# Rotary embedding in an attention stage: partner channels by transfers within SBUF in place of a product with a constant matrix

## The chip, the core and the metric

The kernel runs on one core of a Trainium2 chip. The metric is the time of one execution on the device in microseconds; lower is better. Line numbers are those of the kernel before.

The engines go by their names here: TensorE (PE in the profile) multiplies matrices and writes PSUM, VectorE (DVE) and GpSimd (POOL) work elementwise, ScalarE (ACT) evaluates functions and copies, SyncE (SP) issues most of the DMA transfers. Each engine has one queue and works it in order.

## What is computed

One program runs two blocks of a network on 512 tokens of 1024 channels. The first has an RWKV mixer, a gated delta rule mixer and two dense feed-forward layers. The second has a state-space mixer, a mixture of 32 experts, a dilated windowed attention and a second mixture of 32 experts, each followed by a layer norm. The change lies in the attention. There three groups of eight heads with 64 channels attend in windows; the groups with dilation read the tokens in a strided order. The queries and keys are first rotated in their lowest 16 channels:

```python
def _apply_partial_rope(t, cos, sin):
    half = ROPE_DIM // 2                       # ROPE_DIM = 16 of 64 channels
    t1, t2, rest = t[..., :half], t[..., half:ROPE_DIM], t[..., ROPE_DIM:]
    return jnp.concatenate([t1 * cos - t2 * sin, t2 * cos + t1 * sin, rest], -1)

def _dilated_attention_mixer(x, cos, sin, w_qkv, w_o):
    qkv = (x @ w_qkv).reshape(bsz, s, ATT_N_GROUPS, 3, ATT_HEADS_PER_GROUP, ATT_HEAD_DIM)
    for g, (window, dilation) in enumerate(ATT_PATTERNS):   # (128, 1), (512, 4), (2048, 16)
        q = _apply_partial_rope(qkv[:, :, g, 0], cos, sin)
        k = _apply_partial_rope(qkv[:, :, g, 1], cos, sin)
        o, m, l = _dilated_window_attention(q, k, qkv[:, :, g, 2], window, dilation)
        ...
```

So channel c below 8 needs its partner c + 8 with a minus sign, channel c from 8 to 15 its partner c - 8, and the other 48 channels stay as they are.

## The kernel before

The program is written in a tile framework: the Python code lists instructions in an order, and a scheduler of the framework then places them in the five queues, by the order of the listing and by when it expects operands and buffers to be ready. It also sets all semaphores. Loops are unrolled, except one in each expert layer.

Channels lie on the 128 partitions, so that a tile of 128x512 holds two heads for all 512 tokens. The attention (`attn`, from L1681) makes four passes `proj(p)`, p from 0 to 3, one for each pair of heads in each group. A pass has nine blocks, for the groups 1, 2, 0 in this order, and within each for v, q and k (f = 2, 0, 1). A block is one product of the weights' 128 columns with the 512 tokens, 24 matmuls on TensorE (`block`, the matmuls at L394): weights and tokens are each split into a high and a low part, and three of the four products of parts are kept. ScalarE evicts the finished block to SBUF (`qs`, L1744; L1746 for the group that is not strided). What is done with it is put off into a list `pend` and taken up within the next block, after its third step: for q and k the rotation `rope`, for v four transposes (`vnat`).

A rotation is: a product of the evicted tile with the constant 128x128 matrix `rot` on TensorE, which brings to each channel its partner with the right sign and zero to the others (L1712); a multiplication of the tile by the cosine table on GpSimd (L1715); a multiplication of the product by the sine table on VectorE (L1717) and the sum on VectorE (L1718). Outside the 16 channels the angle is zero. The tables are built once by `rope_tables` on VectorE and ScalarE while the expert layer before ends; two more copies hold them in the strided order (L1705).

`softmax(p)` makes the scores of pass p in four steps: two for the groups 1 and 2 (s = 0), then two for group 0 (s = 1). A step adds the mask (L1760) and the scores (L1767, L1770) in PSUM, takes the maximum on VectorE (L1781), exponentials on ScalarE (L1787), transposes on TensorE (L1797), copies these back on VectorE or ScalarE (L1801, L1799) and multiplies by v (L1812). `merge` lists softmax(p) interleaved with proj(p + 1), in proportion to the costs that the calls are given and that the generators yield.

Between proj(0) and softmax(0) there stands `affine` (L588): the gain and the offset of the last layer norm are applied to the residual, 128x1024 at a time, by eight operations on VectorE (L600), whose gain row is loaded on SyncE's queue (L598) into a buffer of split weights. There too the attention masks are loaded (L336), and VectorE copies them as bf16 (`wmask`, L1882).

Weights come by `Stream`: 512 KB per block on SyncE's queue (L234) into three raw buffers, split by ScalarE (L380) and VectorE (L381) into five buffers each of `wh` and `wl`. A load waits until a split has freed its raw buffer, and a split waits until TensorE has freed its buffer, some blocks ahead of use. Behind the attention's weights the same stream brings those of the second expert layer, whose six further buffers lie where the attention's tiles lay.

Of the kernel before, what the change touches and what calls it, by code (L numbers as in the profile page):

```python
# [9 lines left out]
F32 = mybir.dt.float32  # L10
F32R = mybir.dt.float32r
BF = mybir.dt.bfloat16
I32 = mybir.dt.int32
AF = mybir.ActivationFunctionType
ALU = mybir.AluOpType
# [4 lines left out]
P = 128  # L20
# [264 lines left out]
class Net:  # L285
# [43 lines left out]
        self.gar = c.tile([P, D], F32, name="gar")  # L329
        self.gate = None  # L330

    def load_hc(self, pool, first, end):

        a, b = HC_OFFS[first][0], HC_OFFS[end][0]
        t = pool.tile([P, b - a], F32, name="hc_" + first)
        self.nc.scalar.dma_start(t, self.ins["hc"][:, a:b])  # L336
        for n, (o, w) in HC_OFFS.items():
            if a <= o and o + w <= b and w:
                self.hct[n] = t[:, o - a:o - a + w]
# [1314 lines left out]
    def rope_tables(self, pool, tp):  # L1654

        V, A, nc = self.nc.vector, self.nc.scalar, self.nc
        pi = tp.tile([P, T], I32, name="posi", tag="qs", bufs=2)
        nc.sync.dma_start(pi, bcast_rows(self.ins["positions_2"][0]))
        ang = tp.tile([P, T], F32, name="ang", tag="qs", bufs=2)
        V.tensor_copy(ang, pi)  # L1660
        V.tensor_scalar(ang, ang, self.hcv("freq"), None, op0=ALU.mult)

        k = tp.tile([P, T], F32, name="angk", tag="qr", bufs=2)
        magic = 1.5 * 2.0 ** 23
        V.tensor_scalar(k, ang, 1.0 / (2 * math.pi), None, op0=ALU.mult)
        V.tensor_scalar(k, k, magic, None, op0=ALU.add)
        V.tensor_scalar(k, k, -magic, None, op0=ALU.add)
        rest = 2 * math.pi
        for bits in (5, 13, 21, None):
            c = float(np.float32(rest)) if bits is None else math.floor(rest * 2.0 ** bits) / 2.0 ** bits  # L1670
            rest -= c
            V.scalar_tensor_tensor(ang, k, -c, ang, op0=ALU.mult, op1=ALU.add)
        V.tensor_scalar(ang, ang, 3.1415925, -3.1415925, op0=ALU.min, op1=ALU.max)
        sin, cos = (pool.tile([P, T], F32, name=n) for n in ("sin", "cos"))
        A.activation(sin, ang, AF.Sin)
        V.scalar_tensor_tensor(k, ang, -1.0, ang, op0=ALU.mult, op1=ALU.max)
        V.tensor_scalar(k, k, -1.0, math.pi / 2, op0=ALU.mult, op1=ALU.add)
        A.activation(cos, k, AF.Sin)
        return cos, sin

    def attn(self):  # L1681
# [6 lines left out]
        with self.phase() as pool:  # L1688
# [10 lines left out]
            m4 = lambda a: a.rearrange("p (n b) -> p b n", b=4)  # L1699

            toks = lambda a, i: a[:, i * P:(i + 1) * P]
            tables = [(cos, sin)]
            tables.append([cn.tile([P, T], F32, name=n) for n in ("cos4", "sin4")])
            for a, b in zip(tables[1], tables[0]):
# [2 lines left out]
            def proj(p):  # L1707
                d, pend = X[p], []

                def rope(g, f, qs):  # L1710
                    pr = self.acc()
                    PE.matmul(pr, lhsT=self.hcv("rot"), rhs=qs, start=True, stop=True)  # L1712
                    qc = tp.tile([P, T], F32, name="qr")
                    c, s = tables[g > 0]
                    G.tensor_tensor(qc, qs, c, op=ALU.mult)  # L1715
                    q = d[f, g] = xp.tile([P, T], F32, name=f"qk{f}{g}")
                    V.tensor_tensor(q, pr, s, op=ALU.mult)  # L1717
                    V.tensor_tensor(q, q, qc, op=ALU.add)  # L1718

                def vnat(g, vs):  # L1720
                    pv = self.acc([P, 4, P])
# [5 lines left out]
                for g in (1, 2, 0):  # L1727
                    for f in (2, 0, 1):
                        g_ = self.block()
                        for n in range(NK + 1):  # L1730
                            try:
                                yield next(g_)
                            except StopIteration as e:
                                ps = e.value
                                break
                            if n == 2 and pend:
                                pend.pop()()
                                yield 900
                        while len(pend):
                            pend.pop()()  # L1740
                            yield 900
                        qs = tp.tile([P, T], F32, name="qs")
                        if g:
                            self.last_act = A.activation(qs.rearrange("p (b n) -> p b n", b=4), m4(ps), AF.Copy).ins  # L1744
                        else:
                            self.last_act = A.activation(qs, ps, AF.Copy).ins  # L1746
                        pend.append((lambda g=g, qs=qs: vnat(g, qs)) if f == 2 else (lambda g=g, f=f, qs=qs: rope(g, f, qs)))
                pend.pop()()
                yield 900

            def softmax(p):

# [124 lines left out]

            drain(proj(0))
            self.affine(lambda: self.wsp.tile([P, D], F32, name="row", tag="wl"))
            with self.phase() as p2, self.tc.issue_after(self.last_act):  # L1880
                self.load_hc(p2("at_m"), "attn0", "rot")
                V.tensor_copy(f2(mask), self.hcv("wmask"))  # L1882
            for p in range(4):
                work = [(softmax(p), 4 * 3600)]
                if p < 3:
                    work.append((proj(p + 1), 9 * 6100))
                if p == 2:
                    work.append((combine(0, 2), 10000))
                if p == 3:
# [721 lines left out]
```

## Time and profile before

| | us |
|---|---|
| median of three runs | 3793.52 |
| lowest and highest of these | 3785.03, 3798.27 |
| the profiled execution | 3798.41 |
| span of its instructions | 3796.6 |
| TensorE busy | 3556.3 |
| VectorE busy | 1900.4 |
| ScalarE busy | 1151.8 |
| GpSimd busy | 470.4 |

A profile is of one execution. Busy time of TensorE counts matmuls that overlap, with modelled ends; a busy TensorE is not one at its peak. A row of stretches gives start and end, length, then the busy time and the instructions of PE, PEld (its weight loads), DVE, ACT and POOL, then PEclk, the busy share of the DMA engines and GB/s. "Idle before" of a group is the time in which its engine did nothing just ahead of it. The chain of waits follows the end of a stretch back, at each step to what released the instruction or to the one before it on its engine. PEclk is TensorE's granted clock as a share of 2.4 GHz, the upper of its two levels; the lower is 1.2 GHz.

### The profile page before, as it was taken

What the parts mean: (1) busy time and instruction counts of PE and PEld (TensorE: products, weight loads), DVE (VectorE), ACT (ScalarE), POOL (GpSimd) and SP (SyncE); (2) the same over time, 40 slices, a digit from 0 to 9 for tenths busy, and PEclk for the clock granted to TensorE, in tenths of its full rate; (3) what the DMA queues carried; (4) which work ended last, traced back from release to release, by engine and by line L of the source; (5) the groups of instructions that cost most, each with busy time, mean ns of one, the idle gap of its engine ahead of it and who ended that gap; (6) DMA issues with size and microseconds to landing.
All of it is one profiled execution on the core that took longest, in us unless ns stands there. A gap on an engine that the chain in (4) does not pass through costs nothing. (4 is left out here: it accounts for less than half of the span.)

```text
span 3796.6 us, 53463 instructions
## 1 busy us (share of the span) xinstructions
PE 3556.3 (94%) x21818; PEld 2428.2 (64%) x21818; DVE 1900.4 (50%) x3437; ACT 1151.8 (30%) x2216; POOL 470.4 (12%) x300
## 2 busy tenths in 40 slices
PE   7999998999989998999989998999998999899998
PEld 5766656888776655888868777454546777444443
DVE  6766656533575555644489975222225345322223
ACT  4544433322443333422244432111114333211111
POOL 0111113201111111012131110200001111200001
PEclk9999998999998988999999999999999999899999
DMA  6323343322221102332243453999993224698897
GB/s 235 122 88 122 139 157 134 106 90 99 89 76 40 40 31 65 100 101 89 90 95 112 144 177 124 391 420 375 419 392 93 67 67 151 262 414 329 370 419 298
DMA packets 271342, 676.91 MB, mean 178 GB/s; under 512 B 25549, under 2 KB 164646, under 8 KB 222966
## 3 DMA queue, kind: packets, MB, share of 16 engines
q1 hardware_dynamic: 262342, 667.25, 47.4%
q0 software_dynamic: 928, 3.15, 0.6%
q10 hardware_dynamic: 7824, 3.06, 0.3%
q8 instruction: 173, 2.83, 0.3%
q14 instruction: 75, 0.61, 0.1%
HBM read 660.92 MB, written 12.48 MB: 177 GB/s over the span
## 5 line engine op out<-in xcount | busy, mean ns | idle before, releaser
L381 DVE TENSOR_TENSOR wl<-raw,wh 128x1024 fp32r<-128x1024 f32 x305 | 410.4, 1347 | 407.9 <-ACT wh L380 403.0
L380 ACT ACTIVATE wh<-raw 128x1024 fp32r<-128x1024 f32 x305 | 320.4, 1052 | 807.9 <-PE acc L394 380.1
L394 PE MATMUL acc<-uh,wh 128*128 128x512 f32 x1384 | 558.7, 406 | 2.5 <-ACT uh L380 2.5
L394 PE MATMUL acc<-ul,wh 128*128 128x512 f32 x1384 | 541.3, 391 | 0.0
L394 PE MATMUL acc<-uh,wl 128*128 128x512 f32 x1384 | 540.9, 391 | 0.0
L2083 PE MATMUL acc<-raw,xg 128*64 128x512 f32 x2048 | 449.3, 593 | 7.5 <-DMA raw<-in_moe_w_up_dram 7.5
L2083 PEld LDWEIGHTS acc<-raw,xg 128*64 128x64 f32 x2048 | 147.4, 137 | 300.1 <-issue 275.9
L394 PEld LDWEIGHTS acc<-uh,wh 128*128 128x128 f32 x1384 | 260.8, 189 | 65.5 <-issue 11.3
L394 PEld LDWEIGHTS acc<-ul,wh 128*128 128x128 f32 x1384 | 260.9, 188 | 56.9 <-issue 6.4
L394 PEld LDWEIGHTS acc<-uh,wl 128*128 128x128 f32 x1384 | 260.5, 188 | 56.1 <-issue 0.8
L2083 PE MATMUL acc<-raw,hT 128*64 128x512 f32 x1024 | 233.6, 601 | 3.3 <-issue 2.1
L257 POOL TENSOR_TENSOR raw<-raw,gar 128x1024 f32<-128x1024 f32 x60 | 154.3, 2590 | 616.1 <-DMA raw<-in_ffn_w_out_dram 425.9
L2204 DVE TENSOR_TENSOR h<-h,acc 128x512 f32<-128x512 f32 x32 | 22.0, 688 | 399.9 <-PE acc L2083 399.9
L386 POOL TENSOR_TENSOR rs<-rs,mhalf 128x1 f32<-128x1 f32 x32 | 19.3, 605 | 1169.8 <-DVE rs L385 741.7
L2083 PEld LDWEIGHTS acc<-raw,hT 128*64 128x64 f32 x1024 | 71.9, 138 | 140.6 <-issue 136.9
L2195 DVE SCALAR_TENSOR_TENSOR mrow<-acc,sg,mrow 128x512 fp32r<-128x512 f32 x64 | 47.9, 750 | 199.9 <-ACT mrow L2194 196.6
L394 PE MATMUL tp<-uh,wh 128*128 128x512 f32 x312 | 139.3, 446 | 0.0
L445 PE MATMUL o<-wh,hl 128*128 128x512 f32 x352 | 138.7, 394 | 0.0
L445 PE MATMUL o<-wh,hh 128*128 128x512 f32 x352 | 138.3, 393 | 0.0
L445 PE MATMUL o<-wl,hh 128*128 128x512 f32 x352 | 136.6, 388 | 0.0
L394 PE MATMUL tp<-uh,wl 128*128 128x512 f32 x312 | 134.9, 432 | 0.0
L394 PE MATMUL tp<-ul,wh 128*128 128x512 f32 x312 | 134.6, 431 | 0.0
(664 smaller groups left out, 6235.9 us busy)
## 6 DMA issues: line engine op xcount, KB each, us to landing
raw<-in_moe_w_up_dram SPq DMA_DIRECT2D x128, 1024.0 KB
raw<-in_moe_w_gate_dram SPq DMA_DIRECT2D x126, 1024.0 KB
raw<-in_moe_w_down_dram SPq DMA_DIRECT2D x74, 1024.0 KB
raw<-in_moe_w_down_dram SPq DMA_DIRECT2D x108, 512.0 KB
raw<-in_ada_w_dram SPq DMA_DIRECT2D x48, 1024.0 KB
raw<-in_ffn_w_in_dram SPq DMA_DIRECT2D x44, 1024.0 KB
raw<-in_ffn_w_out_dram SPq DMA_DIRECT2D x20, 1024.0 KB
raw<-in_attn_w_qkv_dram SPq DMA_DIRECT2D x36, 512.0 KB
```

The lines of the kernel that those rows point to most:

```text
L257: n.nc.gpsimd.tensor_mul(src, src, row[:, None, :].to_broadcast(list(src.shape)))
L380: self.nc.scalar.activation(dst_h, src, AF.Copy)
L381: self.last_split = self.nc.vector.tensor_sub(dst_l, src, dst_h.bitcast(F32)).ins
L386: self.pow_ins = self.nc.gpsimd.tensor_tensor(out, out, self.mhalf[:, :out.shape[1]], op=ALU.pow).ins
L394: self.nc.tensor.matmul(ps, lhsT=l[:, k], rhs=r[:, k], start=n == 0, stop=n == 3 * NK - 1)
L445: self.nc.tensor.matmul(ps, lhsT=l[:, kx0 + k, ts], rhs=r[:, k], start=start and n == 0, stop=stop and n == 5)
L2083: self.tc.keep_in_program_order(PE.matmul(*a, **k))
L2195: V.scalar_tensor_tensor(yl[:, cs], y[half], g, yh[:, cs].bitcast(F32), op0=ALU.mult, op1=ALU.subtract)
L2204: V.tensor_tensor(to(h), to(h), of(pu), op=ALU.mult)
```

## The change

The rotation's product with `rot` goes. In its place four transfers on SyncE's queue copy, within SBUF, the 8 partitions of each half of the rotated channels of each head to where the partner is: 8 rows of 512 floats, 16 KB each. Their target is one of two tiles `turned`, cleared once by GpSimd, so that the other channels stay zero. The sign goes into the sine table: the product of `rot` with a column of ones gives each channel's sign, and VectorE multiplies the table by it. The cosine product is written to the result's tile at once, and its own two buffers go. The rotation is no longer put off but listed right behind the eviction, and only v's transposes stay in `pend`. The evicted tile has three buffers, not two; the angles of the tables share them. The masks are loaded into a buffer of the transposed probabilities, not into a pool of their own. The cost given for a pass to `merge` is changed.

```diff
--- before.py
+++ after.py
@@ -329,10 +329,10 @@
         self.gar = c.tile([P, D], F32, name="gar")
         self.gate = None
 
-    def load_hc(self, pool, first, end):
+    def load_hc(self, pool, first, end, **k):
 
         a, b = HC_OFFS[first][0], HC_OFFS[end][0]
-        t = pool.tile([P, b - a], F32, name="hc_" + first)
+        t = pool.tile([P, b - a], F32, name="hc_" + first, **k)
         self.nc.scalar.dma_start(t, self.ins["hc"][:, a:b])
         for n, (o, w) in HC_OFFS.items():
             if a <= o and o + w <= b and w:
@@ -1654,13 +1654,13 @@
     def rope_tables(self, pool, tp):
 
         V, A, nc = self.nc.vector, self.nc.scalar, self.nc
-        pi = tp.tile([P, T], I32, name="posi", tag="qs", bufs=2)
+        pi = tp.tile([P, T], I32, name="posi", tag="qs", bufs=3)
         nc.sync.dma_start(pi, bcast_rows(self.ins["positions_2"][0]))
-        ang = tp.tile([P, T], F32, name="ang", tag="qs", bufs=2)
+        ang = tp.tile([P, T], F32, name="ang", tag="qs", bufs=3)
         V.tensor_copy(ang, pi)
         V.tensor_scalar(ang, ang, self.hcv("freq"), None, op0=ALU.mult)
 
-        k = tp.tile([P, T], F32, name="angk", tag="qr", bufs=2)
+        k = tp.tile([P, T], F32, name="angk", tag="qs", bufs=3)
         magic = 1.5 * 2.0 ** 23
         V.tensor_scalar(k, ang, 1.0 / (2 * math.pi), None, op0=ALU.mult)
         V.tensor_scalar(k, k, magic, None, op0=ALU.add)
@@ -1673,6 +1673,13 @@
         V.tensor_scalar(ang, ang, 3.1415925, -3.1415925, op0=ALU.min, op1=ALU.max)
         sin, cos = (pool.tile([P, T], F32, name=n) for n in ("sin", "cos"))
         A.activation(sin, ang, AF.Sin)
+
+        one, sign = (pool.tile([P, 1], F32, name=n) for n in ("one", "sign"))
+        V.memset(one, 1.0)
+        ps = self.tp([P, 1])
+        nc.tensor.matmul(ps, lhsT=self.hcv("rot"), rhs=one, start=True, stop=True)
+        V.tensor_copy(sign, ps)
+        V.tensor_scalar(sin, sin, sign, None, op0=ALU.mult)
         V.scalar_tensor_tensor(k, ang, -1.0, ang, op0=ALU.mult, op1=ALU.max)
         V.tensor_scalar(k, k, -1.0, math.pi / 2, op0=ALU.mult, op1=ALU.add)
         A.activation(cos, k, AF.Sin)
@@ -1699,6 +1706,11 @@
             m4 = lambda a: a.rearrange("p (n b) -> p b n", b=4)
 
             toks = lambda a, i: a[:, i * P:(i + 1) * P]
+
+            turned = [cn.tile([P, T], F32, name=f"turned{i}") for i in range(2)]
+            for z in turned:
+                G.memset(z, 0.0)
+            turned = itertools.cycle(turned)
             tables = [(cos, sin)]
             tables.append([cn.tile([P, T], F32, name=n) for n in ("cos4", "sin4")])
             for a, b in zip(tables[1], tables[0]):
@@ -1708,14 +1720,15 @@
                 d, pend = X[p], []
 
                 def rope(g, f, qs):
-                    pr = self.acc()
-                    PE.matmul(pr, lhsT=self.hcv("rot"), rhs=qs, start=True, stop=True)
-                    qc = tp.tile([P, T], F32, name="qr")
+                    pr = next(turned)
+                    for r in (0, 64):
+                        for a, b in ((r, r + 8), (r + 8, r)):
+                            nc.sync.dma_start(pr[a:a + 8], qs[b:b + 8])
                     c, s = tables[g > 0]
-                    G.tensor_tensor(qc, qs, c, op=ALU.mult)
                     q = d[f, g] = xp.tile([P, T], F32, name=f"qk{f}{g}")
-                    V.tensor_tensor(q, pr, s, op=ALU.mult)
-                    V.tensor_tensor(q, q, qc, op=ALU.add)
+                    G.tensor_tensor(q, qs, c, op=ALU.mult)
+                    V.tensor_tensor(pr, pr, s, op=ALU.mult)
+                    V.tensor_tensor(q, q, pr, op=ALU.add)
 
                 def vnat(g, vs):
                     pv = self.acc([P, 4, P])
@@ -1739,14 +1752,15 @@
                         while len(pend):
                             pend.pop()()
                             yield 900
-                        qs = tp.tile([P, T], F32, name="qs")
+                        qs = tp.tile([P, T], F32, name="qs", bufs=3)
                         if g:
                             self.last_act = A.activation(qs.rearrange("p (b n) -> p b n", b=4), m4(ps), AF.Copy).ins
                         else:
                             self.last_act = A.activation(qs, ps, AF.Copy).ins
-                        pend.append((lambda g=g, qs=qs: vnat(g, qs)) if f == 2 else (lambda g=g, f=f, qs=qs: rope(g, f, qs)))
-                pend.pop()()
-                yield 900
+                        if f == 2:
+                            pend.append(lambda g=g, qs=qs: vnat(g, qs))
+                        else:
+                            rope(g, f, qs)
 
             def softmax(p):
 
@@ -1877,13 +1891,13 @@
 
             drain(proj(0))
             self.affine(lambda: self.wsp.tile([P, D], F32, name="row", tag="wl"))
-            with self.phase() as p2, self.tc.issue_after(self.last_act):
-                self.load_hc(p2("at_m"), "attn0", "rot")
+            with self.tc.issue_after(self.last_act):
+                self.load_hc(tp, "attn0", "rot", tag="prT")
                 V.tensor_copy(f2(mask), self.hcv("wmask"))
             for p in range(4):
                 work = [(softmax(p), 4 * 3600)]
                 if p < 3:
-                    work.append((proj(p + 1), 9 * 6100))
+                    work.append((proj(p + 1), 9 * 5200 + 3 * 900))
                 if p == 2:
                     work.append((combine(0, 2), 10000))
                 if p == 3:
```

## Rows read from the trace of the kernel before

**Rows 1.** The page: its head, and busy time (share) and instructions by engine.
```profile
span 3796.6 us, 53463 instructions
...
PE 3556.3 (94%) x21818; PEld 2428.2 (64%) x21818; DVE 1900.4 (50%) x3437; ACT 1151.8 (30%) x2216; POOL 470.4 (12%) x300
```

**Rows 2.** Stretches by pass: busy us of each engine, granted clock, DMA share.
```profile
2892.00:2944.00 52.00, 45.27 (x194) 34.67 (x193) 27.88 (x29) 14.02 (x19) 11.07 (x7) 0.96 0.32 96
2944.00:3017.40 73.40, 72.00 (x385) 53.85 (x386) 26.65 (x42) 27.94 (x60) 9.04 (x6) 0.98 0.25 72
3017.40:3089.90 72.50, 71.91 (x395) 54.10 (x394) 27.89 (x51) 26.90 (x60) 10.39 (x7) 1.00 0.22 66
3089.90:3166.80 76.90, 76.90 (x461) 57.57 (x460) 36.05 (x63) 26.77 (x60) 11.43 (x7) 1.00 0.27 86
```

**Rows 3.** Groups by line, 2892 to 3166: count, busy us, mean ns, idle before.
```profile
L1715 POOL TENSOR_TENSOR qr<-qs,cos 128x512 f32<-128x512 f32 x24 | 41.4, 1727 | 237.6 <-ACT qs L1744 156.0 <-ACT qs L1746 63.5 <-DVE cst L1840 18.0
...
L1712 PE MATMUL acc<-qs,hc_rot 128*128 128x512 f32 x47 | 25.0, 611 | 3.4 <-ACT qs L1746 3.4
...
L1718 DVE TENSOR_TENSOR qk<-qk,qr 128x512 f32<-128x512 f32 x23 | 15.9, 690 | 1.6
L1717 DVE TENSOR_TENSOR qk<-acc,sin 128x512 f32<-128x512 f32 x23 | 15.8, 687 | 13.9 <-PE acc L1712 13.9
```

**Rows 4.** Chain of waits, 2892 to 2945: start, length, what stood on it.
```profile
2894.57 0.86 PE acc L1712 x2
...
2919.54 0.86 PE acc L1712 x2
...
2923.87 3.68 DMA row<-in_ln_g_dram
...
2943.97 1.03 PE acc L1760 x2
```

**Rows 5.** Chain of waits, 2944 to 3164: shares by line.
```profile
by line: PE acc L394 69.3%; PE acc L1712 7.2%; PE po L1812 5.2%; PE tp L1797 4.5%; PE acc L1767 3.4%; PE acc L1760 2.7%; PE acc L1770 2.6%; PE acc L1865 1.9%; PE acc L1723 1.8%; issue 0.7%; ACT qs L1746 0.5%; ACT wh L380 0.2%
```

**Rows 6.** TensorE's waits, 2944 to 3164: total us, times, longest.
```profile
PE acc L1760 <- DVE wmask L1882: 5.3, 1, 5.3
PE acc L1712 <- ACT qs L1746: 2.0, 2, 1.4
```

**Rows 7.** SyncE's DMA issues in order of time: early in the span, and near 3201.
```profile
275.04 0.33 SPq L1034 DMA_DIRECT2D od<-yT  x1
...
277.07 0.32 SPq L1040 DMA_DIRECT2D oback<-od  x1
...
3201.07 1.28 SPq L234 DMA_DIRECT2D raw<-in_moe_w_gate_dram  x3
```

**Rows 8.** Waits of SyncE's queue, 2850 to 3260: total us, times, longest.
```profile
SPq L234 <- DVE wl L381: 275.6, 38, 13.5
```

**Rows 9.** Timeline of pass three: first head's exponentials (ACT) and transposes (PE), two steps.
```profile
3021.52 0.47 ACT L1787 ACTIVATE pr<-acc,stat 128x256 f32<-128x256 f32 x1
...
3035.11 0.46 ACT L1787 ACTIVATE pr<-acc,stat 128x256 f32<-128x256 f32 x1
...
3025.12 0.60 PE L1797 MATMUL tp<-hc_ident,pr 128*128 128x128 f32 x4
...
3042.77 0.60 PE L1797 MATMUL tp<-hc_ident,pr 128*128 128x128 f32 x4
```

**Rows 10.** Line L1677: count, min/median/max ns, when.
```profile
L1677 DVE TENSOR_SCALAR angk<-angk x1: 430/430/430, 2881.0 to 2881.0; 128x512 f32<-128x512 f32 x1
```

**Rows 11.** Chain of waits behind the last block, 3155 to 3185.
```profile
3168.59 0.70 DVE qk L1718
3169.28 1.20 DVE stat L1781 x2
```

**Rows 12.** A stretch ahead of the experts, and the first expert product on TensorE.
```profile
3236.00:3246.00 10.00, 2.55 (x24) 2.33 (x23) 7.45 (x36) 0.42 (x2) 0.00 (x0) 0.50 0.00 1
...
3246.53 0.55 PE L2083 MATMUL tp<-mrow,ul 128*128 128x256 f32 x1 [1.96 <-DVE mrow L2088]
```


## The prediction

> **What bounds the kernel now.** First the page: the span is 3796.6 us in an execution of 3798.41 us, and TensorE is busy 94% of it, VectorE 50%, GpSimd 12% [rows 1]. Such a share is a mean over stages, so the next view is the table of stretches, cut where the attention stage starts a new pass [rows 2]. Attention runs from 2892 to about 3167 us. In its three passes with softmax beside projection (2944 to 3167) TensorE is busy 72.0 of 73.4, 71.9 of 72.5 and 76.9 of 76.9 us, at a granted clock of 0.98 to 1.00, which is the upper level of 2.4 GHz; VectorE has 27 to 36 us of work there and the DMA engines are a quarter full. In the first pass (2892 to 2944), which has no softmax beside it, TensorE is busy 45.3 of 52.0. So three passes are bound by TensorE, and work taken off it there shortens the kernel, while the first pass has another limit at its end. The chain of waits says the same and names the lines: for 2944 to 3164 it stands on TensorE nearly throughout, with 7.2% on L1712, the rotation product [rows 5]. For the first pass it goes along TensorE until 2923.87, then through the load of the norm's gain row (3.68 us) and VectorE, which applies gain and offset rows to the residual (eight operations), and comes back to TensorE at 2943.97 by way of the mask copy [rows 4].
>
> **What is removed.** 24 rotation products, six in each of four passes. The profile shows two records per product, of 0.61 us each [rows 3], but matmuls overlap; what one costs is its step on the chain, 0.86 us for its two records [rows 4]. In the first pass four of the six stand on the chain, 0.86 us each (the first and the last are shown), ahead of the gain row's load: 4 x 0.86 = 3.4 us. The load waits for a buffer that TensorE releases, so it moves with them. The last two stand beside VectorE's work and are worth nothing. In the three later passes the chain's own sum is 7.2% of the 220 us from 2944 to 3164, 15.8 us; this is 17 products, since the last one of pass four lies behind 3164. At the end of two of these passes TensorE also waits for the eviction that the last product reads, 2.0 us [rows 6]; the next instruction will be the mask product of the next scores, whose rotated channels come three blocks earlier. That makes 3.4 + 15.8 + 2.0 = 21.2 us.
>
> **What is added and moved.** (1) 96 transfers of 16 KB on SyncE's queue, four per rotation. No transfer within SBUF is in this trace. The nearest from below: a 256 KB store is issued at 275.04, and a load that reads it back follows at 277.07, after a wait, so landing takes 2.0 us with its issue [rows 7]. From above: the 512 KB gain row, 3.68 us [rows 4]. Issues follow each other by 1.28 / 3 = 0.43 us [rows 7]. So the last of four lands 3 x 0.43 + 2.0 = 3.3 us after the eviction, at most 1.3 + 3.7 = 5.0. I take 3.3, because a transfer of 16 KB is nearer to the smaller neighbour. With two VectorE operations of 0.69 us [rows 3] the rotated tile is there 4.7 to 6.4 us after its eviction. The first scores of a pass read groups 1 and 2, whose last rotation is three blocks (over 16 us of TensorE) earlier, and group 0 is read two score steps later still: the latency itself is hidden by projection work. If that cover were gone, it would cost its 4.7 us once per pass, 19 us.
> (2) SyncE works in order. A rotation's transfers wait for ACT's eviction; behind them stand weight loads, which now wait 275.6 us in all for VectorE's split to free a buffer [rows 8]. Splits run up to four blocks ahead of their use, so 1.7 us of issues in front of a load, 40 us in all, are covered. The other way round is worse: a load waiting for a split ahead of a rotation's transfers holds these back. In passes two to four splits follow evictions within about 1 us. At the end of pass one splits stand among the residual's work, and a rotation held there would hold the mask copy behind it.
> (3) VectorE keeps two operations per rotation. The first now reads SBUF alone; SBUF alone costs 690 ns and PSUM with SBUF 687 [rows 3], so nothing. But it waits for DMAs instead of TensorE, and behind it on VectorE may stand the maximum of the scores, which releases ACT's exponentials and then TensorE's transposes. In pass three the first head's exponentials end at 3021.99 and its transposes start at 3025.12, 3.1 us of slack; in the next step it is 3035.57 and 3042.77, 7.2 us [rows 9]. The longer slack covers even 5.0 us. The shorter one stands at the start of a pass, right behind the last rotation of the pass before. There VectorE would begin the maximum 3.3 + 1.4 = 4.7 us after that eviction, where TensorE's scores no longer wait for it; against 3.1 us of slack TensorE loses 1.6 us, in passes three and four together 3.2, if VectorE's order puts the rotation first, and nothing if it puts the maximum first. I take 2 us; the late end is 2 x (1.6 + 1.7) = 6.6.
> (4) GpSimd's multiplication stays the same, 1.73 us [rows 3] against one rotation every 12 us. Its two clearings of 128x512 come before the first rotation; GpSimd has almost nothing there.
> (5) The tables: one multiplication of the sine table by a sign, 0.43 us like L1677 [rows 10], a copy of one column and a one-column product. VectorE is on the chain there, so 0.6 us; between 0 and 2, if VectorE waits for the product among TensorE's other work.
> (6) Releasing the fifth accumulator, a third buffer for the evicted tile, and the planner's cost of 5200 for 6100 per block change no duration; they may shift where softmax work falls in between, less than a score step's slack either way.
> (7) Exit: behind the last block VectorE does the last rotation's two operations ahead of the score maximum, on the chain [rows 11]. If the maximum goes first, 1.3 us are won; if VectorE waits for the last transfer ahead of it, up to 1.4 are lost. I take zero.
> (8) The expert stage behind attention begins with its buffers full: DMA is idle from 3236 to 3246, and TensorE then waits for VectorE's one-hot rows, not for weights [rows 12]. All loads of that stage are released by what runs before them, so the gain is passed on whole.
>
> Sum: 21.2 - 2.0 - 0.6 = 18.6 us. From the profiled execution: 3798.4 - 18.6 = 3779.8. That execution lies 4.9 us over the median of the runs, 3793.5; the forecast for the median is 3775. Its own range is 3768 (all of 21.2 and 1.3 at the exit, with some scatter) to 3782 (21.2 less the late ends: 6.6, 2 and 1.4).
>
> The Trainium skill (DMA: Bandwidth & Descriptors, Rules for kernel authors) speaks against this change: many small transfers should be coalesced, since under 64 KB one pays mostly overhead. Its fixed cost of about 2 us per DMA (Anatomy of one DMA — SWDGE (gpsimd) path, stated for that queue) paid four times in a row would be an estimate of 8 us per rotation; no transfer within SBUF here shows it. By that rule the sum would turn over, as the last rival shows; the rows of issues that follow each other by 0.43 us speak for overlap [rows 7].
>
> **Rivals.** *The gain is mostly hidden, 3785, chance 0.20.* At the end of pass one SyncE has a load ahead that waits for a split behind the residual's work. The last rotation then comes after VectorE has done it, and the mask copy later: instead of winning 3.4 us, pass one loses about 4 (landing 3.3 and 0.7 for the operation), and the starts of passes three and four cost 5 rather than 2. That is 18.6 - 3.4 - 4 - 3 = 8 us left. For it: TensorE already waits 5.3 us there for the mask [rows 6]. Against it: TensorE reaches the last eviction some 5 us earlier, while VectorE's residual work takes as long as before, so the transfers have time.
> *Transfers held behind the next weight load, slower, 3841, chance 0.07.* Place: SyncE's queue in passes two to four, with each rotation's transfers ordered behind the load that waits for the next split. Price: a block lasts 72.5 / 9 = 8.1 us, so a rotation comes 8.1 + 2.0 = 10.1 us after its eviction, and VectorE, held all that time, has 27.9 + 6 x 10.1 = 88.5 us per pass of 72.5 [rows 2] and is the bound: 3 x 16 = 48 us slower. It decides from a hold of (72.5 - 5.2 - 27.9) / 6 = 6.6 us per rotation on, since 5.2 us is what TensorE saves per pass. For it: the queue already waits 275.6 us for splits [rows 8]. Against it: a rotation's transfers are ready a little before that split, so an order by readiness puts them first.
> *The four transfers go one after the other, slower, 3806, chance 0.04.* Then a rotation takes 4 x 2.03 = 8.1 us [rows 7], VectorE has 27.9 + 6 x 8.1 = 76.5 us per pass and again is the bound: 3 x 4.0 = 12 us slower. The rule of the skill above would be its ground.
> *The change doesn't do what it says* is not open for the products, which are gone from the program; it could only be that TensorE's order around them falls worse, which is in the range.
>
> **How the numbers follow.** Forecast 0.69, hidden 0.20, the two slower ones 0.11. Differences under 0.3%, 11.4 us, can't be told from none in this kernel. The forecast's range (11 to 26 us won) is faster: 0.69. The hidden case is within: 0.20. The rest is slower: 0.11. The range of 8 in 10 takes in forecast and hidden case with the runs' scatter of a few us: 3765 to 3795.
>
> **What would show it.** Right: L1712 is gone; TensorE stays busy over 98% of passes two to four, which last 5 to 6 us less each; the expert stage begins 18 us earlier and lasts as long; a rotation's transfers land 3 to 5 us after its eviction. Wrong: TensorE idle ahead of the transposes or the score products with VectorE named as the releaser; VectorE waiting long for the transfers; TensorE's wait for the mask far over 7 us. An end of attention earlier by 18 us with no gain at the end of the kernel would refute step (8).

## The result, and the profile after

The kernel after takes 3774.5 us (median of 20 runs, 3759.2 to 3798.3) against 3794.9 us for the kernel before, run beside it (20 runs, 3785.0 to 3809.2): a ratio of 0.995, 95% interval 0.9936 to 0.9964. The forecast was 3775. The profiled execution took 3775.04 us. Line numbers in the views below are those of the kernel that the view is of. First the page of the kernel after, the span and the busy time of the engines, which answers to [rows 1].

```profile
span 3773.2 us, 53604 instructions
...
PE 3530.8 (94%) x21772; PEld 2418.9 (64%) x21772; DVE 1902.0 (50%) x3440; ACT 1151.2 (31%) x2216; POOL 469.5 (12%) x302
```

TensorE has 46 records and 25.5 us less; VectorE and GpSimd are as before. The span is 23.4 us shorter, and not all of that is the change. TensorE's timeline shows in both traces where the last product of the expert layer before ends, where the first projection product and the mask products that open a pass stand, and where the first product of the expert layer behind attention stands. Cut there, the kernel after is 5.4 us ahead when attention begins (at 2853.42 and at 2848.06), wins 20.8 us in the attention stage, and takes 2.8 us longer in the experts behind it (550.1 and 552.8 us). The change does not touch the code of the first and the third stretch, and their lengths scatter by more than that among the runs below (2840 to 2870 us and 548 to 555 us). So the stage is the measure: 393.1 us before, 372.3 after.

Stretches of the kernel after, from mask product to mask product, with the columns of [rows 2]: stretch and length, busy time of PE, PEld, DVE, ACT, POOL, granted clock, DMA share, GB/s. The first is pass one.

```profile
2887.89:2934.89 47.00, 39.36 (x180) 32.23 (x178) 27.76 (x26) 13.77 (x19) 10.77 (x7) 0.97 0.40 115
2934.89:3002.43 67.54, 67.54 (x374) 52.16 (x375) 29.13 (x44) 26.53 (x59) 7.79 (x5) 0.97 0.28 80
3002.43:3068.10 65.67, 65.67 (x376) 50.88 (x375) 29.41 (x48) 26.75 (x60) 9.64 (x6) 1.00 0.28 79
3068.10:3139.10 71.00, 71.00 (x447) 54.96 (x446) 35.05 (x64) 28.02 (x62) 9.94 (x6) 1.00 0.29 88
```

In passes two to four TensorE has no idle time left: busy time equals length. Its clock is at the upper level but for the start of pass two, behind TensorE's wait at the end of pass one. The granted clock is 0.50 there, the lower level, for 3.16 us of work in the kernel before and for 4.20 us in the kernel after:

```profile
2943.97:2947.13 3.16, 3.16 (x19) 2.10 (x20) 1.16 (x2) 0.00 (x0) 0.00 (x0) 0.50 0.75 221
```

```profile
2934.89:2939.09 4.20, 4.20 (x21) 2.95 (x22) 4.10 (x6) 0.00 (x0) 0.00 (x0) 0.50 0.44 127
```

The four passes cut at the same events in the kernel before lasted 51.72, 73.91, 72.52 and 76.21 us. For the sum, the three passes and the exit are cut at the last projection product instead (3164.90 and 3139.26), before above and after below:

```profile
2943.97:3164.90 220.93, 218.93 (x1231) 164.35 (x1231) 89.60 (x151) 81.02 (x179) 29.73 (x17) 0.99 0.24 75
3164.90:3246.53 81.63, 66.43 (x452) 52.81 (x450) 48.52 (x135) 29.48 (x61) 10.44 (x9) 0.84 0.34 131
```

```profile
2934.89:3139.26 204.37, 204.37 (x1195) 158.12 (x1196) 93.74 (x154) 81.31 (x179) 27.37 (x17) 0.99 0.29 83
3139.26:3220.37 81.11, 65.36 (x450) 52.54 (x447) 48.11 (x136) 29.35 (x61) 10.28 (x9) 0.82 0.37 141
```

The passes are 16.6 us shorter: TensorE's busy time by 14.56 us, and its idle time by 2.00, from 2.00 to nothing. The chain of waits of 2935 to 3139, beside [rows 5], has lost L1712 and has no other engine on it at all:

```profile
by line: PE acc L394 75.8%; PE po L1826 5.6%; PE tp L1811 4.9%; PE acc L1781 3.7%; PE acc L1774 2.9%; PE acc L1784 2.8%; PE acc L1879 2.0%; PE acc L1736 1.9%; PE tp L1858 0.4%
```

The rotation itself, 2880 to 3140: GpSimd's product with the cosine, VectorE's two operations (count, busy us and mean ns, idle time ahead), answering to [rows 3].

```profile
L1729 POOL TENSOR_TENSOR qk<-qs,cos 128x512 f32<-128x512 f32 x23 | 37.5, 1631 | 216.6 <-ACT qs L1757 162.1 <-ACT qs L1759 54.5
L1730 DVE TENSOR_TENSOR turned<-turned,sin 128x512 f32<-128x512 f32 x23 | 17.0, 738 | 36.4 <-DMA turned<-qs 36.4
L1731 DVE TENSOR_TENSOR qk<-qk,turned 128x512 f32<-128x512 f32 x23 | 17.0, 738 | 2.1 <-DVE turned L1730 0.5
```

VectorE now waits 36.4 us for the transfers and TensorE for none of that. How soon they land is seen where VectorE waits for one: the eviction on ACT (start, length), the four issues on SyncE's queue, VectorE's operation with its wait in brackets.

```profile
2905.77 0.58 ACT L1757 ACTIVATE qs<-acc 128x512 f32<-128x512 f32 x1
```

```profile
2906.37 2.68 SPq L1726 DMA_DIRECT2D turned<-qs  x4
```

```profile
2910.50 0.69 DVE L1730 TENSOR_TENSOR turned<-turned,sin 128x512 f32<-128x512 f32 x1 [3.38 <-DMA turned<-qs]
```

From the eviction's end, 2906.35, to 2910.50 is 4.15 us (4.14 for the next one that waits). The issues follow each other by 2.68 / 4 = 0.67 us.

The end of pass one, the chain of waits (start, length), answering to [rows 4]:

```profile
2923.19 0.65 SPq L1726
...
2925.24 1.94 DMA turned<-qs
...
2927.59 4.57 DVE res L600 x3
2932.16 0.60 DVE turned L1730
...
2934.42 0.42 DVE wmask L1896
...
2934.89 1.04 PE acc L1774 x2
```

It ends as before, with the residual's operations, a rotation and the mask copy on VectorE. The chain also leads through a rotation's transfers (2923.19 to 2927.19), but they were no limit: VectorE was at work until 2927.6, and the pass is as long without them (no_transfers below). TensorE's wait there, and those of SyncE's queue (2850 to 3260: total us, times, longest), answering to [rows 6, 8]:

```profile
PE acc L1774 <- DVE wmask L1896: 7.6, 1, 7.6
```

```profile
SPq L234 <- DVE wl L381: 93.4, 17, 13.0
SPq L1726 <- ACT qs L1757: 76.6, 16, 8.3
```

The queue waits less for splits (275.6 us in [rows 8]), and it now waits for evictions as well.

### The profile page after: what moved, and what is told of

Same layout as the page of the kernel before. It is cut to its first block, busy times and chain, and to the rows that moved or that the text cites. A ratio compares the mean times of both kernels' runs of the same rounds, so it can differ in the third digit from the quotient of the medians.

```text
span 3773.2 us, 53604 instructions
## 1 busy us (share of the span) xinstructions
PE 3530.8 (94%) x21772; PEld 2418.9 (64%) x21772; DVE 1902.0 (50%) x3440; ACT 1151.2 (31%) x2216; POOL 469.5 (12%) x302
## 5 line engine op out<-in xcount | busy, mean ns | idle before, releaser
L2097 PE MATMUL tp<-mrow,ul 128*128 128x256 f32 x512 | 130.3, 294 | 4.0 <-DVE mrow L2102 4.0
```

The source lines that it names most:

```text
L2097: self.tc.keep_in_program_order(PE.matmul(*a, **k))
```

## The experiments

Attention by stretch in each profile, in us, cut at the same events. "Prologue" runs from the last expert product of the layer before to the first projection product, "exit" from the mask product that follows pass four to the first expert product.

| kernel | prologue | pass 1 | pass 2 | pass 3 | pass 4 | exit | stage | ratio to before, 95% |
|---|---|---|---|---|---|---|---|---|
| before | 38.8 | 51.7 | 73.9 | 72.5 | 76.2 | 79.9 | 393.1 | 1 |
| after | 39.8 | 47.0 | 67.5 | 65.7 | 71.0 | 81.3 | 372.3 | 0.9936 to 0.9964 |
| no_product | 38.1 | 47.0 | 67.6 | 65.5 | 71.0 | 81.8 | 370.9 | 0.9910 to 0.9958 |
| no_transfers | 39.4 | 46.9 | 67.3 | 65.7 | 71.0 | 81.2 | 371.4 | 0.9926 to 0.9971 |
| transfers_twice | 42.9 | 42.6 | 67.5 | 65.7 | 71.0 | 82.1 | 371.7 | 0.9912 to 0.9972 |
| product_too | 39.7 | 51.5 | 75.1 | 72.3 | 76.2 | 80.6 | 395.4 | 1.0002 to 1.0034 |
| two_queues | 40.1 | 46.6 | 67.7 | 65.7 | 71.0 | 81.1 | 372.2 | 0.9940 to 0.9976 |
| rows_four | 39.7 | 42.9 | 67.2 | 65.7 | 71.0 | 82.0 | 368.5 | 0.9919 to 0.9950 |
| mask_early | 40.8 | 39.2 | 69.3 | 65.7 | 71.0 | 81.1 | 367.0 | 0.9893 to 0.9945 |
| mask_and_queues | 42.9 | 39.2 | 69.2 | 65.7 | 71.0 | 81.0 | 368.9 | 0.9906 to 0.9952 |
| after_again | 40.5 | 47.3 | 67.5 | 65.7 | 71.0 | 81.2 | 373.1 | 0.9910 to 0.9953 |
| mask_early_again | 42.9 | 39.2 | 68.9 | 65.7 | 71.0 | 81.3 | 368.9 | 0.9917 to 0.9952 |
| transfers_four | 40.3 | 42.9 | | | | | 427.8 | 1.0082 to 1.0130 |

**Is it the product?** First the kernel before with the product left out, so that the sine term reads the evicted tile itself; its output lacks the swap of partner channels.

```
-                    pr = self.acc()
-                    PE.matmul(pr, lhsT=self.hcv("rot"), rhs=qs, start=True, stop=True)
...
-                    V.tensor_tensor(q, pr, s, op=ALU.mult)
+                    V.tensor_tensor(q, qs, s, op=ALU.mult)
```

> The kernel before without the rotation product (VectorE multiplies the evicted tile by the sine table in place of its partner, so the rotation is wrong; all else as before). Attention stage here: from the last product of the first expert layer to the first of the second, 393.1 us before, 372.3 after the change. Theory (the gain is TensorE's time for the products plus its waits at the passes' ends): stage 372 +- 2, time about 21 us under the kernel before. Rival (the gain comes from listing the rotation earlier, or from the fifth accumulator being free): stage stays above 385.

The passes are those of the kernel after within 0.2 us, with no transfer, no sign in the table and no third buffer, and with the rotation listed where it was. The accumulator that the product wrote is free here too, and no run separates the two; but in passes two to four of the kernel before TensorE waited for nothing except the evictions that the product reads, 2.0 us [rows 6], so there was no wait for an accumulator to win. Then the reverse: the kernel after, with the product run beside the transfers and its result unused.

```
                             rope(g, f, qs)
+                            pend.append(lambda qs=qs: PE.matmul(self.acc(), lhsT=self.hcv("rot"), rhs=qs, start=True, stop=True))
+                while len(pend):
+                    pend.pop()()
+                    yield 900
```

> The changed kernel with the product of the evicted tile and the constant matrix kept on TensorE beside the transfers, put off into the next block as before; nobody reads it. Theory: 0.86 us for each of the 21 or so that stand on the chain, so 18 to 22 us of the gain are lost, stage 390 to 395. Rival (the product was hidden, the gain came otherwise): stage within 5 us of 372.3.

All of the gain is gone: 75.1, 72.3 and 76.2 us, and the chain of 2948 to 3170 has the product's share back (L1764 is its line here; 7.2% in [rows 5]). The stage, 395.4 us, is 0.4 over my figure. That pass two is 1.2 us longer than before goes with the clock: the granted clock is 0.50 for its first 6.0 us, not for 3.2.

```profile
by line: PE acc L394 69.5%; PE acc L1764 7.1%; PE po L1830 5.2%; PE tp L1815 4.5%; PE acc L1785 3.4%; PE acc L1778 2.7%; PE acc L1788 2.6%; PE acc L1736 2.0%; PE acc L1883 1.8%; issue 0.7%; ACT qs L1759 0.5%; ACTq L1759 0.0%
```

**What do the transfers cost?** The kernel after without them (the partner tile stays zero), and with each of them issued twice.

```
-                    for r in (0, 64):
-                        for a, b in ((r, r + 8), (r + 8, r)):
-                            nc.sync.dma_start(pr[a:a + 8], qs[b:b + 8])
```

> The changed kernel without the 96 transfers (the turned tiles stay zero, so the sine part is left out). Theory (transfers are hidden except ahead of the mask copy at the end of pass one and at the exit): stage 4 to 6 us shorter than the changed kernel's 372.3, so 366 to 368; passes two to four 67.1, 65.7, 71.0 us from score product to score product change by under 1 us each. Rival (VectorE's 36 us of waiting for the transfers costs something in every pass): each of these passes 3 us shorter or more, stage 360 or less.

```
-                    for r in (0, 64):
+                    for r in (0, 64, 0, 64):
```

> The changed kernel with each of the four transfers made twice, so eight issues of 0.67 us and a landing of 1.9 us: the rotation waits 7.3 us for its partner, not 4.6. Theory (slack covers it inside the passes; the two ends pay 2.7 us each): stage 372.3 + 3 to 8, passes two to four within 1.5 us each. Rival (as the prediction had it: from a hold of 6.6 us per rotation VectorE becomes the bound, 27.9 + 6 x 7.3 = 71.7 us per pass): passes two to four 5 us longer each or more, stage 388 or more.

Without transfers the stage is 0.9 us shorter, about what the kernel after differs from itself (372.3 and 373.1); I had expected 4 to 6, so the holds that I priced are not there. With twice as many I had expected 3 to 8 us more; the stage is 0.6 shorter, although a rotation's partner now comes 7.1 us after its eviction. VectorE's wait for them (2885 to 3140) did not double, it fell:

```profile
DVE turned L1730 <- DMA turned<-qs: 9.8, 7, 3.8
```

VectorE's order had been made anew, with more of its other work ahead of each rotation. That shows in pass one too, where the residual's operations went behind the mask copy: VectorE has 13 us of work there, not 28, and 38 in pass two, not 29, and pass one is 4.4 us shorter.

```profile
2888.89:2931.53 42.64, 39.33 (x179) 32.22 (x178) 12.97 (x15) 13.77 (x19) 9.52 (x7) 1.00 0.38 96
2931.53:2998.99 67.46, 65.85 (x375) 50.87 (x375) 38.07 (x53) 27.20 (x59) 8.29 (x6) 1.00 0.39 105
```

Passes three and four are unchanged. Pass two has the length of the kernel after (67.5 us) by chance: its clock is at the upper level throughout, so that TensorE is busy for 1.7 us less, but it idles for 1.6 us. The chain of waits leads from there through an eviction, which stands on ScalarE behind the split of a late weight load, to the transfers ahead of that load on SyncE's queue. So the doubled transfers did cost something once, by the queue and not by VectorE:

```profile
2934.93 0.62 SPq L1726
...
2936.10 5.68 DMA raw<-in_attn_w_qkv_dram
...
2942.82 0.59 ACT qs L1757
...
2943.46 0.66 PE acc L1736 x4
```

Two more of this kind: half of the transfers issued by ScalarE, and each cut into two of four rows, which doubles the issues and not the bytes.

```
-                    for r in (0, 64):
+                    for q_, r in ((nc.sync, 0), (nc.scalar, 64)):
...
-                            nc.sync.dma_start(pr[a:a + 8], qs[b:b + 8])
+                            q_.dma_start(pr[a:a + 8], qs[b:b + 8])
```

> The kernel after, with two of the four small transfers of each rotation issued by ScalarE and two by SP. Theory (the transfers lie beside TensorE's other work): the partner is there some 1.3 us sooner after the eviction (two issues of 0.67 us fewer on SP), which nothing waits for; ScalarE, busy a third of the time, issues 48 transfers more; passes two to four stay at 67.5, 65.7 and 71.0 us within 0.5 us, and the time is the kernel after's within 0.1%, ratio 0.994 to 0.996. Rival (the late partner still costs TensorE something in the passes): they get shorter by up to 6 x 1.3 us each, ratio 0.990 or less. Other rival: ScalarE's issues delay the exponentials and evictions behind them, and the passes get longer by 1 to 2 us each.

```
-                            nc.sync.dma_start(pr[a:a + 8], qs[b:b + 8])
+                            for o in (0, 4):
+                                nc.sync.dma_start(pr[a + o:a + o + 4], qs[b + o:b + o + 4])
```

> The kernel after with each small transfer of 8 rows cut into two of 4 rows: the same bytes, 192 issues instead of 96. If SP's 0.62 us is the price of an issue, each still takes about 0.62 us, a rotation's partner is there 8 x 0.67 + 1.9 = 7.3 us after the eviction, SP is as busy as with every transfer issued twice, and the passes stay at 67.5, 65.7 and 71.0 us within 0.5 us (ratio 0.994 to 0.996), since TensorE waits for none of it. Rival (the price goes by rows or bytes): an issue takes 0.31 us, and the partner is there 4.6 us after the eviction as in the kernel after.

Neither moves any of passes two to four by more than some 0.3 us, though the partner comes 3.1 us after its eviction in the first and 6.4 us in the second. An issue of four rows takes nearly what one of eight takes, 5.07 / 8 = 0.63 us, so the price goes by the issue, and the rival (0.31 us) is out:

```profile
2948.01 5.07 SPq L1727 DMA_DIRECT2D turned<-qs  x8
```

Pass one is shorter in rows_four as in transfers_twice, again with the residual's work put behind.

**Where do they begin to cost?** Each issued four times, 16 per rotation (`for r in (0, 64) * 4:`).

> The kernel after, with every small transfer issued four times (16 a rotation, 384 in all). One rotation's transfers then take about 16 x 0.67 + 1.9 = 12.7 us from the eviction, and SP issues transfers for 6 x 10.7 = 64 us in a pass of 66 to 71 us, beside its weight loads. Theory (there is a point at which the transfers come onto the path, and it is SP's time to issue, not VectorE's hold): weight loads come late, TensorE waits for weights, and the passes get longer by 5 to 15 us each; stage 385 to 415 us, ratio 1.000 to 1.010. Rival (VectorE's holds, 12.7 us in a rotation period of 8 to 11 us, make VectorE the bound, as the rival of the forecast had it from 6.6 us on): passes longer by 6 x 6 = 36 us each, stage 480 us or more, ratio 1.02 or more. Other rival (even this is hidden): passes within 1 us of the kernel after's.

Slower than before: 3839.9 us against 3798.0. Pass boundaries mix in this kernel; from the first to the last projection product it takes 284.5 us (251.4 in the kernel after), and behind that 103.0 (81.1). The stage, 427.8 us, is 13 over the upper end of my figure, because the exit suffered too, and far below the 480 of the rival. SyncE's queue is full: it takes 16 transfers, then one or two weight loads, then 16 again. Its most frequent wait (2900 to 3292, second view) is for the transfers themselves: each is issued again to the same rows, and the next issue waits for the one before it to land.

```profile
3007.21 12.82 SPq L1726 DMA_DIRECT2D turned<-qs  x16
3020.07 0.44 SPq L234 DMA_DIRECT2D raw<-in_attn_w_qkv_dram  x1
```

```profile
SPq L1726 <- DMA turned<-qs: 29.4, 22, 2.0
```

The chain of waits of 3000 to 3292 runs through it, 18.6% on these issues, with late weight loads behind them:

```profile
3030.54 0.62 SPq L1726
...
3033.03 5.22 DMA raw<-in_attn_w_qkv_dram
3038.27 1.06 ACT wh L380
```

So the point is SyncE's queue, which the transfers hold for about 12 us of every 13 here; 16 x 0.67 = 10.7 of these are issues, and the rest is mostly the wait for landings, which only the repetition brings. TensorE's waits are mixed: up to 3230 those for rotated tiles sum to 8.9 us, those for evicted blocks of v to 8.4 and those for split weights to 3.6. Its granted clock falls too: over the projections it is 0.94, and TensorE idles for 18.1 us and is busy for 267.1 (7.6 and 243.7 in the kernel after):

```profile
2902.70:3187.84 285.14, 267.08 (x1388) 203.19 (x1386) 113.44 (x178) 93.02 (x198) 34.86 (x24) 0.94 0.31 80
```

VectorE itself waits 68.4 us for the transfers in the stage. How much each of these costs was not separated.

**The wait that is left.** The largest wait of TensorE in the stage is the 7.6 us for the mask, with the lower clock behind it. The load and copy of the mask constants were written ahead of pass one; once alone, once with two_queues, and once more beside the kernel after.

```
+            self.load_hc(tp, "attn0", "rot", tag="prT")
+            V.tensor_copy(f2(mask), self.hcv("wmask"))
             drain(proj(0))
...
-            with self.tc.issue_after(self.last_act):
-                self.load_hc(tp, "attn0", "rot", tag="prT")
-                V.tensor_copy(f2(mask), self.hcv("wmask"))
```

> The kernel after, with the load of the mask constants and their copy on VectorE written ahead of the first pass instead of behind it. Theory: in the kernel after TensorE waits 7.6 us for the mask at the end of pass one, because the copy stands on VectorE behind the rotations and the residual's work, and the load behind the last eviction. With the mask there early TensorE goes on at once: pass one 47.0 -> 40 to 42 us, the attention stage 372.3 -> 365 to 368 us, the time 5 to 7 us below the kernel after (3768 to 3770 us, ratio to before 0.993). Rival: the wait only changes its name (VectorE, late with the residual and the gain rows, holds the first maxima of the scores): pass one gets shorter but the pass behind it longer, the stage gains under 2 us, 3773 to 3775 us.

> Both edits together: the mask constants loaded ahead of pass one, and half of the small transfers issued by ScalarE. Theory: the gain of the early mask alone, 5 to 7 us below the kernel after, plus at most 1.3 us at the end of pass one, where the last rotation waits for its transfers: 3766 to 3770 us, stage 364 to 368 us. Rival: the stage as in the kernel after (372 us), because VectorE's residual work ends the pass in either.

> The kernel after, unchanged, beside the next kernel on one chip, so that the two can be set against each other. Expected: ratio to the kernel before 0.994 to 0.996, attention stage 372 us, TensorE's wait for the mask 7 to 8 us.

> The kernel after with the load of the mask constants and its copy written ahead of the first pass, once more, beside the kernel after on one chip. The stage of the profile was 5.3 us shorter with it (366.99 against 372.31 us). Theory (that is a gain of its own): 4 to 6 us below the kernel after, ratio to before 0.992 to 0.994. Rival (the gain is in this stage but is lost behind it, or was scatter): within 2 us of the kernel after.

The first two passes of mask_early, and TensorE's waits in them:

```profile
2905.84:2945.01 39.17, 39.17 (x180) 32.22 (x178) 19.86 (x18) 12.26 (x18) 9.60 (x6) 1.00 0.40 116
2945.01:3014.28 69.27, 65.86 (x375) 50.75 (x375) 36.46 (x51) 27.92 (x61) 9.18 (x6) 1.00 0.31 87
```

```profile
PE tp L1811 <- ACT pr L1801: 3.4, 1, 3.4
```

Pass one loses its idle time and is 7.8 us shorter. TensorE idles for 3.4 us in pass two instead, where the first exponentials wait for a maximum that stands behind the residual's work on VectorE. The same products, though, are done there in 65.86 us and not in 67.54: without the wait at the end of pass one the clock stays at its upper level (1.00, against 0.97), which gives back 1.7 us. The stage is 5.3 us shorter in one profile and 4.3 in the other (368.9 against 373.1); with two_queues it is 368.9, a little over my figure. In time that is 3770.0 us in one comparison and, beside the kernel after, 3771.9 against 3775.0; the intervals lie on each other, so a gain of this size is seen in the stage and not shown in the time. The prologue came out at 38 to 41 us in most profiles and at 42.9 in three of the early-mask and doubled kernels; why is open.

## Why the prediction was right, and which sizes were off

| step | forecast, us | measured, us |
|---|---|---|
| products ahead of the end of pass one | -3.4 | -4.7 |
| 17 products, passes two to four | -15.8 | -14.6 |
| TensorE's waits at pass ends | -2.0 | -2.0 |
| (3) holds at the starts of passes three and four | +2.0 | 0 |
| (5) tables | +0.6 | +1.0 (prologue; not clear of its scatter) |
| (7) exit | 0 | -0.5 |
| sum | -18.6 | -20.8 |

The measured column is the stretches above: 51.72 less 47.00, busy and idle time of the three passes, the prologue, 81.63 less 81.11. The prologue took 39.8 and 40.5 us in two profiles of the kernel after, and 40.8 and 42.9 in two of the early mask, so its 1.0 is not shown to be the tables. The mechanism is shown from both sides: leaving out the product alone brings the whole gain, and adding it back to the new kernel takes the whole gain away. The product stood on an engine that had nothing idle beside it; its successor stands on engines that had.

That the median came within 0.5 us of the forecast is partly luck. The kernel before ran 1.4 us above the median that the forecast started from, the gain was 1.8 us larger than forecast, and in the table errors of -1.3, +1.2, -2.0, +0.4 and -0.5 us offset each other in part. The interval of the ratio allows a gain of 14 to 24 us, so the time cannot tell one of these sizes from another.

**The products.** The chain's 7.2% gave 15.8 us, and TensorE's busy time lost 14.6. A part of the difference is the clock, which the sum left out: the kernel after has 1.04 us more of work at the lower level at the start of pass two (4.20 and 3.16 us), and as the 4.20 us cost 1.68 against mask_early, that is some 0.4 us (an estimate). That 14.6 is also 17 times the step of 0.86 is therefore no confirmation. The rest was not traced.

**Step (1).** The partner is there 4.1 us after the eviction, not 3.3, inside the bound of 5.0: an issue takes 0.67 us from one to the next, where I had read 0.43 off weight loads. Here the Trainium skill (DMA: Bandwidth & Descriptors, Rules for kernel authors), that under 64 KB one pays mostly overhead, agrees with the trace: 16 KB take 1.94 us from the start of an issue to landing, almost as long as the 2.0 us of a 256 KB store [rows 7]. The traces decide against what I made of it as a rival: four such transfers land within 4.1 us and not 8, and left out altogether they change no pass by more than 0.3 us.

**Step (3)** failed. It took the last rotation of a pass to stand ahead of the first maximum on VectorE. At the start of pass three of the kernel after it stands behind:

```profile
3004.63 1.28 DVE L1795 TENSOR_REDUCE stat<-acc 128x2 f32<-128x512 f32 x2
...
3008.04 0.69 DVE L1730 TENSOR_TENSOR turned<-turned,sin 128x512 f32<-128x512 f32 x1 [1.92 <-DMA turned<-qs]
```

The exponentials are done at 3007.9, the transposes come at 3008.98, and the wait of 1.92 us falls into time in which VectorE had nothing else. This was the "nothing if it puts the maximum first" of the step; I took a value nearer to the other end.

**Pass one.** The mask was the limit, as forecast, and TensorE's wait for it grew to 7.6 us (about 7 was forecast). But a second thing moved. In the kernel before both last rotations stood on VectorE ahead of the mask copy; in the kernel after the last one stands behind it:

```profile
2941.17 0.68 DVE L1717 TENSOR_TENSOR qk<-acc,sin 128x512 f32<-128x512 f32 x1
...
2942.90 0.68 DVE L1718 TENSOR_TENSOR qk<-qk,qr 128x512 f32<-128x512 f32 x1
2943.50 0.41 DVE L1882 CAST wmask<-hc_attn 128x512 bf16<-128x512 f32 x1
```

```profile
2934.42 0.41 DVE L1896 CAST wmask<-hc_attn 128x512 bf16<-128x512 f32 x1
...
2937.03 0.68 DVE L1730 TENSOR_TENSOR turned<-turned,sin 128x512 f32<-128x512 f32 x1
```

From the start of the residual's operations to the mask product it is 16.4 us before (2927.58 to 2943.97) and 14.3 after (2920.59 to 2934.89), 2.1 won. The residual itself began only 2.6 us sooner in the pass, not 3.4 (35.3 and 32.7 us after the first projection product). The order alone does not make the gain: no_product keeps both rotations ahead of the copy and has the same 47.0 us (the residual 31.7 us after the first projection product, then 15.3), and product_too has the order of the kernel after and 51.5 (36.0, then 15.4). What tells the short passes from the long ones is the product.

**The rivals.** The hidden gain didn't come: the mask copy went ahead of the last rotation, pass one won 4.7 us, and the starts of passes three and four cost TensorE nothing. Transfers held behind a weight load didn't come either: where VectorE waits for a partner, it comes 4.1 us after its eviction. The formula in it, that VectorE is the bound from a hold of 6.6 us per rotation on, is refuted: at 7.1 us passes three and four did not change, and at four times the transfers SyncE was full before VectorE was. It took every hold as time in which VectorE has nothing else to do; its order fills it. Four transfers one after the other would have taken 8.1 us. The step that passes the gain on whole, (8), agrees with the time: 20.4 us between the medians, 20.8 in the stage.

## What to carry to other kernels

An operation on the engine that bounds a stage is worth its step on the chain of waits times its count, even when what replaces it takes five times as long, provided that nothing reads the result soon and that the engines and queues which take it over have idle time: look at the distance from the eviction to the first reader, not at the latency alone. Price the replacement by the queue that issues it (here 0.67 us for each small transfer on SyncE): that queue also feeds the weights, and it was late first, for one load at eight transfers per rotation and throughout at sixteen. Before costing a hold on an in-order engine, look at what its order can put ahead of it. And before calling a difference in busy time work, compare the granted clock: here a wait of 7.6 us at the end of one pass cost 1.7 us more in the next.

## What the runs showed of the hardware beyond that

A transfer of 8 rows within SBUF occupies SyncE's queue for 0.62 us and one of 4 rows for 0.58, where the issue of a 512 KB weight load shows 0.39 us. Four of 8 rows are there 4.1 us after they may start and eight of 4 rows 6.4 us, so their landings overlap with the next issues and the issues set the rate. The 7.1 us of the doubled transfers are no such figure: the fifth waits 0.9 us for the first to land, because it writes the same rows.
